# Half of the second MLP layer's outputs by Strassen's seven block products, with tokens as rows, in turn with ordinary output chunks

## The chip, the core and the metric

The kernel runs on one core of a Trainium2 chip. The metric is the time of one execution on the device in microseconds (us); shorter is better. The engines are named as the profile names them: TensorE (PE; its weight loads PEld), VectorE (DVE), ScalarE (ACT), GpSimd (POOL) and SyncE (SP), which issues the loads.

## The reference

Two layers of a decoder trunk over 256 tokens of width 2048, all in float32. Each layer has a mixer (layer 0: a convolution module beside differential attention; layer 1: a gated short convolution), a cross-attention into 256 memory tokens, and the MLP that the change touches:

```python
D_MODEL, SEQ, DEPTH, D_FF = 2048, 256, 2, 4 * 2048

def sq_relu_mlp(h, w1, w2):
    return jnp.square(jax.nn.relu(h @ w1)) @ w2

for l in range(DEPTH):
    x = x + (even_mixer if l % 2 == 0 else odd_mixer)(rms_norm(x, mix_norm_g[l]), ...)
    x = x + cross_attention(rms_norm(x, xattn_norm_g[l]), mem_n, ...)
    x = x + sq_relu_mlp(rms_norm(x, mlp_norm_g[l]), mlp_w1[l], mlp_w2[l])
return rms_norm(x, final_norm_g)
```

## The kernel before

**Layout.** The residual `x` stays in SBUF with channels as partitions: 16 tiles of 128 channels by 256 tokens. A matrix product makes one *output chunk* at a time, 128 output channels by 256 tokens, over 16 input tiles (`proj_long`, L191, and its kin).

**Three products for one.** Matmuls run on a rounded format (float32r), so each operand is split in a rounded part *hi* and a remainder *lo*, and a product is hi·hi + hi·lo + lo·hi. For weights, `weights` (L152) loads a raw tile of 128 x 1024 (512 KB) on SyncE's queue, ScalarE casts it to hi (L163), VectorE subtracts hi from raw into lo (L164). Activations lie as hi and lo next to each other (`Act`, L229), 512 columns for 256 tokens. An output chunk is 16 matmuls of a hi weight block against those 512 columns and 16 of a lo weight block against the 256 hi columns; the weight block is stationary. `residual` (L322) then adds the two halves of the PSUM bank to `x` with two VectorE additions (L325).

**Tokens as rows.** `proj_rows` (L213) does it the other way round: a 128x128 block of activations is stationary and 512 weight columns stream past it; every matmul has 512 columns.

**MLP.** `mlp` (L713) runs in four quarters of 2048 hidden units, in each of two layers, so eight in all. A quarter has 16 chunks of the first layer (each followed by the sum of its halves L209/L210, the relu and scale L720, the square L722, and the split into hi and lo, chunk by chunk, L245/L246) and 16 chunks of the second layer over these 16 tiles of hidden units, each added to `x`. In the last quarter `residual` also prepares the next norm.

**Order and buffers.** The program is unrolled; a scheduler fixes each engine's order before the run, and inserts the semaphores. Each engine works strictly in its order; a flag (`strict`) holds TensorE to the order of the program text. Tiles with the same tag share a number of slots: 5 for raw weights (`wraw`), 3 each for hi and lo weights (`wspl`), 13 large activation slots (`half`: with 4 each for the normed input and two sets of hidden units, 12 in use in the MLP). PSUM has 8 banks: 4 for chunks (`ps_mm`), 3 for attention (`ps_at`), 1 for norms (`ps_nm`).

Of the kernel before, what the change touches and what calls it, by code (L numbers as in the profile page):

```python
# [10 lines left out]
F32 = mybir.dt.float32  # L11
# [6 lines left out]
P = 128  # L18
# [27 lines left out]
def trunk(ctx: ExitStack, tc: tile.TileContext, d):  # L46
# [8 lines left out]
    prob = ctx.enter_context(tc.tile_pool(name="prob", bufs=4))  # L55
    tmp = ctx.enter_context(tc.tile_pool(name="tmp", bufs=2))
    small = ctx.enter_context(tc.tile_pool(name="small", bufs=4))
    ps_mm = ctx.enter_context(tc.tile_pool(name="ps_mm", bufs=4, space=bass.MemoryType.PSUM))
# [36 lines left out]
    def load_vec():  # L95
        nc.sync.dma_start(out=vec, in_=d["vec"][:, NG:])
        lv = vec[:, VEC["lam"] - NG:VEC["lam"] - NG + 256].rearrange("p (a b) -> p a b", a=4)
        lp = tmp.tile([P, S], F32, tag="t32", name="lp", bufs=7)[:, :128].rearrange("p (a b) -> p a b", a=2)
# [20 lines left out]
    def ordered(i, token):  # L119

        tc.stamp_issue_order_token(i.ins, token)
# [20 lines left out]
    def mm(*a, **k):  # L142
        i = T.matmul(*a, **k)  # L143
        if strict[0]:
            ordered(i, "pe")
# [3 lines left out]
        if strict[0]:  # L149
            ordered(i, "pe")  # L150

    def weights(src):  # L152
        run_later(rate[0], calls[0])
        run_stages(calls[0])
        calls[0] += 1
        raw = wraw.tile([P, 1024], F32, tag="raw", name="raw")
        hi = wspl.tile([P, 1024], F32R, tag="whi", name="whi")
        lo = wspl.tile([P, 1024], F32R, tag="wlo", name="wlo")
        n = 512 if calls[0] == 1 else 1024
        for i in range(0, 1024, n):  # L160
            o = slice(i, i + n)
            nc.sync.dma_start(out=raw[:, o], in_=src[:, o])
            A.copy(hi[:, o], raw[:, o])  # L163
            ordered(V.tensor_tensor(lo[:, o], raw[:, o], f(hi[:, o]), op=ALU.subtract), "lo")  # L164
        return hi, lo

    def wide_piece(ps, hi, lo, act, k, first, last):
# [20 lines left out]
                wide_piece(ps, hi, lo, act, g * 8, first, last)  # L188
        return pp

    def proj_long(src, act):  # L191

        ps = ps_mm.tile([P, 512], F32, tag="mm", name="mm")
        (h0, l0), (h1, l1) = [weights(src[:, g * 1024:(g + 1) * 1024]) for g in range(2)]
# [11 lines left out]
    def summed(ps):  # L206

        t = tmp32("sum")
        A.copy(t, ps[:, S:])  # L209
        V.tensor_tensor(t, ps[:, :S], t, op=ALU.add)  # L210
        return t
# [58 lines left out]
    def spread(rows):  # L270
        ps = ps_nm.tile([P, 512], F32, tag="nm", name="nmb")[:, :S]
        for t in range(2):
            dg = tmp.tile([P, P], F32, tag="diag", name="diag")
# [21 lines left out]
        return y  # L295

    def to_sbuf(ps, pool=None, name="rb"):
        r = pool.tile([P, S], F32, tag=name, name=name) if pool else tmp.tile([P, S], F32, tag="rb", name=name, bufs=3)
        A.copy(r, ps)
        return r  # L300

# [15 lines left out]
            V.tensor_tensor(self.acc, self.acc, sq, op=ALU.add)  # L317

    def tmp32(name="t32"):
        return tmp.tile([P, S], F32, tag="t32", name=name, bufs=7)  # L320

    def residual(k, ps, nxt, ss, gname):  # L322

        for i in range(2):
            V.tensor_tensor(x[:, k], x[:, k], ps[:, i * S:(i + 1) * S], op=ALU.add)  # L325
# [13 lines left out]
        return softmax_from(src, nm, width, scale)  # L339

    def softmax_from(src, bias, width, scale):
        p = tmp.tile([P, S], F32, tag="pexp", name="pexp", bufs=4)
# [9 lines left out]
    def even_mixer():  # L352
# [77 lines left out]
        def turn(h, pr):  # L430
            pt = ps_at.tile([P, 512], F32, tag="at", name="ptd")
            for t in range(2):
                for kt in range(t + 1):
                    o = kt * S + t * P
                    transpose(out=pt[:, o:o + P], in_=pr[t, 0][0][:, kt * P:(kt + 1) * P], identity=ident)
            ahl = prob.tile([P, 2, 512], F32R, tag="pt", name="ahl")
# [42 lines left out]
        def head(h):  # L479
            mem_piece(m, mss, h)  # L480
            if h == H1 - 1:
                stage(4, mem_rows)
            qkt = prob.tile([P, 2, 2, S], F32R, tag="pt", name="dqk")
# [5 lines left out]
        lsum = tmp.tile([P, S], F32, tag="lsum", name="lsum", bufs=1)  # L489

        def gated(c):
            av = summed(proj(w[c], xa))
# [149 lines left out]
    def cross(l, xa, ss, kmem):  # L642
# [20 lines left out]
        def turn(h, pr, v):  # L663
            pt = ps_at.tile([P, 512], F32, tag="at", name="ptx")
            for t in range(2):
                for kt in range(2):
                    transpose(out=pt[:, kt * S + t * P:kt * S + (t + 1) * P], in_=pr[t][:, kt * P:(kt + 1) * P],
                              identity=ident)
            pb = prob.tile([P, 2, 512], F32R, tag="pt", name="pb")
# [40 lines left out]
        return nxt, nss  # L710


    def mlp(l, xa, ss, gname):  # L713
        r = rstd(ss.acc, D)
        nxt = nss = None
        for qd in range(4):
            hid = Act(NC, "hid")
            for c in range(NC):
                u = summed(proj_long(d[f"w1{l}"][qd * NC + c], xa))
                V.scalar_tensor_tensor(u, u, 0.0, r, op0=ALU.max, op1=ALU.mult)  # L720
                u2 = tmp32("u2")
                A.activation(u2, u, AF.Square)  # L722
                hid.put(c, u2)
            if qd == 3:
                nxt, nss = Act(NC, "xn") if l == 0 else None, SumSq()
            for c in range(NC):
                ps = proj_long(d[f"w2{l}"][c][:, qd * D:(qd + 1) * D], hid)
                residual(c, ps, nxt, nss, gname)
        return nxt, nss

    xa, ss, kmem = even_mixer()
    xa, ss = cross(0, xa, ss, kmem)
    xa, ss = mlp(0, xa, ss, "mix1")
    xa, ss, kmem = odd_mixer(xa, ss)
    xa, ss = cross(1, xa, ss, kmem)
    _, ss = mlp(1, xa, ss, "final_norm_g")

    r = spread(rstd_rows(ss.acc, D))
    for g in range(8):
# [63 lines left out]
```

## Time and profile before

| | before |
|---|---|
| median of 3 runs | 2913.12 us (2912.9 to 2913.8) |
| the profiled execution | 2913.22 us, its span 2911.4 us |
| VectorE busy | 2006.7 us (69%) |
| ScalarE busy | 1471.6 us (51%) |
| DMA moved | 540.03 MB, mean 185 GB/s |
| mean granted TensorE clock | 0.998 |

How to read it: the span runs from the first to the last instruction of one execution; the profiled execution's own time is 1.8 us longer. Busy time is the time in which an engine executed instructions. In lines of groups the columns are: line, engine, operation, output<-inputs, shapes, count, then total busy us, mean ns of one, and the idle time ahead of them with what ended it. In windows they are: the window, its length, and for PE, PEld, DVE, ACT and POOL the busy us and the count, then the granted clock, the share of the DMA engines' time, and GB/s. In timelines and in the chain of waits they are: start, length, engine, line and what. Lines of DMA issues end in KB and in the median us from issue to landing.

### The profile page before, as it was taken

What the parts mean: (1) busy time and instruction counts of PE and PEld (TensorE: products, weight loads), DVE (VectorE), ACT (ScalarE), POOL (GpSimd) and SP (SyncE); (2) the same over time, 40 slices, a digit from 0 to 9 for tenths busy, and PEclk for the clock granted to TensorE, in tenths of its full rate; (3) what the DMA queues carried; (4) which work ended last, traced back from release to release, by engine and by line L of the source; (5) the groups of instructions that cost most, each with busy time, mean ns of one, the idle gap of its engine ahead of it and who ended that gap; (6) DMA issues with size and microseconds to landing.
All of it is one profiled execution on the core that took longest, in us unless ns stands there. A gap on an engine that the chain in (4) does not pass through costs nothing.

```text
span 2911.4 us, 42713 instructions
## 1 busy us (share of the span) xinstructions
PE 2891.9 (99%) x16536; PEld 2544.3 (87%) x16536; DVE 2006.7 (69%) x3180; ACT 1471.6 (51%) x2181; POOL 3.9 (0%) x20
## 2 busy tenths in 40 slices
PE   9999999999999999999999999999999999999998
PEld 7888888898888888888888888888988888888887
DVE  7899987767666656566777765467676666565665
ACT  6766455555544535445544444455555445354453
POOL 0000000000000000000000000000000000000000
PEclk9999999999999999999999999999999999999999
DMA  7464565545565665656656656655455656656564
GB/s 251 157 199 164 186 196 186 172 147 181 186 191 188 190 190 188 192 188 189 184 194 197 203 193 195 193 188 171 139 188 188 188 189 189 190 189 191 188 189 137
DMA packets 150395, 540.03 MB, mean 185 GB/s; under 512 B 16688, under 2 KB 16816, under 8 KB 150192
## 3 DMA queue, kind: packets, MB, share of 16 engines
q1 hardware_dynamic: 150192, 537.30, 58.0%
q8 instruction: 130, 2.13, 0.3%
q14 instruction: 73, 0.60, 0.1%
HBM read 535.13 MB, written 2.10 MB: 185 GB/s over the span
## 4 chain that ended last, share of the span: by engine, by line
PE 99%; DVE 0%; DMA 0%; ACT 0%; issue 0%; DVEq 0%; SPq 0%; ACTq 0%
PE mm L143 89%; PE mmr L143 8%; PE pox L143 1%; PE sx L143 1%; PE nmb L143 0%; PE nmr L143 0%; PE sc L143 0%; PE po L143 0%; DVE x L741 0%; PE ptx L148 0%; DMA x<-xT 0%; PE ptd L148 0%; ACT xn L255 0%; DVE x L325 0%; DVEq L798 0%
## 5 line engine op out<-in xcount | busy, mean ns | idle before, releaser
L164 DVE TENSOR_TENSOR wlo<-raw,whi 128x1024 fp32r<-128x1024 f32 (+1 forms) x1009 | 1234.2, 1223 | 718.6 <-issue 318.3
L163 ACT CAST whi<-raw 128x1024 fp32r<-128x1024 f32 (+1 forms) x1009 | 1061.6, 1052 | 721.3 <-PE mm L143 594.0
L143 PE MATMUL mm<-xn,whi 128*128 128x512 f32 x3840 | 937.0, 392 | 0.0
L143 PEld LDWEIGHTS mm<-xn,whi 128*128 128x128 f32 x3840 | 702.0, 188 | 133.2
L143 PEld LDWEIGHTS mm<-xn,wlo 128*128 128x128 f32 x3840 | 500.7, 191 | 23.8
L143 PE MATMUL mm<-xn,wlo 128*128 128x256 f32 x3840 | 508.4, 282 | 0.0
L143 PE MATMUL mm<-hid,whi 128*128 128x512 f32 x2048 | 489.8, 391 | 0.0
L143 PEld LDWEIGHTS mm<-hid,whi 128*128 128x128 f32 x2048 | 377.0, 188 | 72.8
L209 ACT COPY sum<-mm 128x256 f32<-128x256 f32 x272 | 101.2, 372 | 604.6 <-PE mm L143 604.4
L143 PEld LDWEIGHTS mm<-hid,wlo 128*128 128x128 f32 x2048 | 262.6, 191 | 10.0
L143 PE MATMUL mm<-hid,wlo 128*128 128x256 f32 x2048 | 265.7, 283 | 0.0
L210 DVE TENSOR_TENSOR sum<-mm,sum 128x256 f32<-128x256 f32 x272 | 115.2, 423 | 105.3 <-ACT sum L209 104.8
L325 DVE TENSOR_TENSOR x<-x,mm 128x256 f32<-128x256 f32 x384 | 160.6, 418 | 14.6 <-PE mm L143 7.9
L143 PE MATMUL mmr<-whi,mem 128*128 128x512 f32 x512 | 137.3, 390 | 0.0
L143 PE MATMUL mm<-mem,whi 128*128 128x512 f32 x512 | 126.3, 393 | 0.0
L143 PE MATMUL mm<-o,whi 128*128 128x512 f32 x512 | 124.7, 392 | 0.0
L505 DVE SCALAR_TENSOR_TENSOR cv<-a,vec,cv 128x255 f32<-128x255 f32 (+14 forms) x240 | 111.4, 464 | 2.9
L143 PEld LDWEIGHTS mmr<-whi,mem 128*128 128x128 f32 x512 | 95.8, 188 | 19.6
L143 PEld LDWEIGHTS mm<-o,whi 128*128 128x128 f32 x512 | 93.7, 188 | 18.6 <-DVE o L252 0.9
L143 PEld LDWEIGHTS mm<-mem,whi 128*128 128x128 f32 x512 | 93.1, 188 | 17.3
L143 PE MATMUL mmr<-wlo,mem 128*128 128x512 f32 x256 | 78.8, 389 | 0.0
L143 PEld LDWEIGHTS mm<-mem,wlo 128*128 128x128 f32 x512 | 67.6, 190 | 3.8
(165 smaller groups left out, 1780.2 us busy)
## 6 DMA issues: line engine op xcount, KB each, us to landing
raw<-w SPq DMA_DIRECT2D x512, 512.0 KB, 3.9
raw<-odd_in SPq DMA_DIRECT2D x96, 512.0 KB, 4.4
raw<-even_in SPq DMA_DIRECT2D x64, 512.0 KB, 4.3
raw<-xk SPq DMA_DIRECT2D x64, 512.0 KB, 4.2
raw<-xv SPq DMA_DIRECT2D x64, 512.0 KB, 3.6
raw<-xq SPq DMA_DIRECT2D x64, 512.0 KB, 4.0
raw<-xo SPq DMA_DIRECT2D x64, 512.0 KB, 3.9
raw<-even_out SPq DMA_DIRECT2D x32, 512.0 KB, 4.2
```

The lines of the kernel that those rows point to most:

```text
L143: i = T.matmul(*a, **k)
L163: A.copy(hi[:, o], raw[:, o])
L164: ordered(V.tensor_tensor(lo[:, o], raw[:, o], f(hi[:, o]), op=ALU.subtract), "lo")
L209: A.copy(t, ps[:, S:])
L210: V.tensor_tensor(t, ps[:, :S], t, op=ALU.add)
L325: V.tensor_tensor(x[:, k], x[:, k], ps[:, i * S:(i + 1) * S], op=ALU.add)
L505: ordered(V.scalar_tensor_tensor(cv[:, c, s:], a[:, c, :S - s], col("conv_a_w", i + j), cv[:, c, s:], op0=ALU.mult, op1=ALU.add), "lo")
```

## The change

In six of the eight quarters (the first three of each layer) the 16 second-layer chunks are made in another way. The eight chunks of the upper half of the channels (8 to 15) stay as they were. The 1024 channels of the lower half are computed with tokens as rows by the Strassen–Winograd scheme of seven block products. The matrix of 256 tokens x 2048 hidden units is cut in 2 x 2 blocks (128 tokens; even and odd tiles of hidden units), the weights in 2 x 2 blocks (even and odd tiles; two halves of 512 columns). Each of eight steps takes one pair of hidden tiles: seven products, each of three matmuls of 512 columns (hi·hi, lo·hi, hi·lo), 21 in all, into seven PSUM banks that stay open over all eight steps. After each step comes one ordinary chunk, in the eighth bank (`ps_nm`); TensorE is held to this order.

What belongs to it:

- the hidden units are split into hi and lo four chunks at a time, and `SevenAct.combine` forms and splits the sums and differences of their blocks;
- `seven_weights` loads the weights of a step in two tiles, in runs of 1 KB, and forms and splits the weight blocks, five of seven of them sums or differences; three of its tiles (`b22`, `tw`) have one slot;
- `seven_sum` adds the seven banks to `x` at the end of a quarter;
- `turned` transposes the lower half of `x` to token rows before the first quarter's second layer and back in the last quarter;
- in the ordinary chunks between steps, the lo part of the second half of the weights is not made by VectorE: ScalarE writes -raw, rounded, and a DMA issued by GpSimd adds the weights onto it from DRAM;
- some buffers shrink: `t32` 7 to 6 slots, `rb` 3 to 2, `diag` 2 to 1, `pexp` 4 to 3; the tiles that only the attention uses live in a pool opened around it, and the MLP's new tiles in one around the MLP.

The core of the diff:

```diff
-    def weights(src):
+    def weights(src, added=False):
...
             nc.sync.dma_start(out=raw[:, o], in_=src[:, o])
             A.copy(hi[:, o], raw[:, o])
-            ordered(V.tensor_tensor(lo[:, o], raw[:, o], f(hi[:, o]), op=ALU.subtract), "lo")
+            if added:
+                A.activation(lo[:, o], raw[:, o], AF.Copy, scale=-1.0)
+                G.dma_start(out=lo[:, o], in_=src[:, o], accum_op=ALU.add)
+            else:
+                ordered(V.tensor_tensor(lo[:, o], raw[:, o], f(hi[:, o]), op=ALU.subtract), "lo")
...
-    def proj_long(src, act):
+    def proj_long(src, act, ps=None, added=False):
...
+        (h0, l0), (h1, l1) = [weights(src[:, g * 1024:(g + 1) * 1024], added and g == 1) for g in range(2)]
...
+    class SevenAct:
+        def __init__(self, act):
+            self.act = act
+            self.t = [half.tile([P, 2, 4, 2, P], F32R, tag="half", name="hs") for _ in range(4)]
+
+        def combine(self, j, u):
+            a11, a21, a12, a22 = [u[:, :, i] for i in range(4)]
+            V.tensor_tensor(a22, a21, a22, op=ALU.add)
+            V.tensor_tensor(a21, a11, a21, op=ALU.subtract)
+            V.tensor_tensor(a11, a22, a11, op=ALU.subtract)
+            V.tensor_tensor(a12, a12, a11, op=ALU.subtract)
+            t = self.t[j]
+            A.copy(t[:, :, :, 0], u)
+            V.tensor_tensor(t[:, :, :, 1], u, f(t[:, :, :, 0]), op=ALU.subtract)
...
+    def seven_weights(src):
+        raw = [wraw.tile([P, 4, 2, P], F32, tag="raw", name="raws") for _ in range(2)]
+        for i, t in enumerate(raw):
+            nc.sync.dma_start(out=t.rearrange("p c k f -> p c (k f)"),
+                              in_=src[4 * i:4 * i + 4].rearrange("c p f -> p c f"))
+        b1, b2 = [t.rearrange("p c k f -> p k c f") for t in raw]
+        sh = wspl.tile([P, 2, 4, P], F32R, tag="whi", name="shi")
+        sl = wspl.tile([P, 2, 4, P], F32R, tag="wlo", name="slo")
+        bt = pools["mlp"].tile([P, 2, 4, P], F32R, tag="b22", name="b22", bufs=1)
+        t1, t2 = [pools["mlp"].tile([P, 2, 2, 4, P], F32R, tag=f"tw{i}", name="tw", bufs=1) for i in range(2)]
+        A.copy(sh, b1)
+        V.tensor_tensor(sl, b1, f(sh), op=ALU.subtract)
+        V.tensor_tensor(b1[:, 0], b2[:, 0], b1[:, 0], op=ALU.subtract)
+        A.copy(bt[:, 0], b2[:, 1])
+        V.tensor_tensor(b2[:, 0], b2[:, 1], b2[:, 0], op=ALU.subtract)
+        V.tensor_tensor(bt[:, 1], b2[:, 1], f(bt[:, 0]), op=ALU.subtract)
+        V.tensor_tensor(b2[:, 1], b2[:, 1], b1[:, 0], op=ALU.subtract)
+        V.tensor_tensor(b1[:, 1], b2[:, 1], b1[:, 1], op=ALU.subtract)
+        for t, b in ((t1, b1), (t2, b2)):
+            A.copy(t[:, 0], b)
+            V.tensor_tensor(t[:, 1], b, f(t[:, 0]), op=ALU.subtract)
...
+    def seven_step(pp, src, sa, s, first, last):
+        b = seven_weights(src)
+        for i, a, w in ((1, sa.single(2 * s, 0), "b11"), (2, sa.single(2 * s + 1, 0), "b21"),
+                        (5, sa.comb(1, s), "t1"), (4, sa.single(2 * s + 1, 1), "t4"), (3, sa.comb(4, s), "b22"),
+                        (7, sa.comb(3, s), "t3"), (6, sa.comb(2, s), "t2")):
+            mm(pp[i], a[0], b[w][0], start=first, stop=False)
+            mm(pp[i], a[1], b[w][0], start=False, stop=False)
+            mm(pp[i], a[0], b[w][1], start=False, stop=last)
+
+    def seven_sum(pp, acc):
+        (c11, c12), (c21, c22) = [[acc[:, i, j * 512:(j + 1) * 512] for j in range(2)] for i in range(2)]
+        u = pools["mlp"].tile([P, 512], F32, tag="u", name="u", bufs=2)
+        A.copy(u, pp[1])
+        for out, other, op in ((c11, u, ALU.add), (c11, pp[2], ALU.add), (c12, pp[5], ALU.add),
+                               (c22, pp[5], ALU.add), (c21, pp[4], ALU.subtract), (c12, pp[3], ALU.add),
+                               (u, pp[6], ALU.add), (c12, u, ALU.add), (u, pp[7], ALU.add), (c21, u, ALU.add),
+                               (c22, u, ALU.add)):
+            V.tensor_tensor(out, out, other, op=op)
+
+    def turned(rows):
...
+        for i, bank in enumerate(banks):
+            for j in range(4):
...
+                transpose(out=bank[:, j * P:(j + 1) * P], in_=src, identity=ident)
+        for i, bank in enumerate(banks):
+            A.copy(chan[:, 2 * i:2 * i + 2].rearrange("p k s -> p (k s)"), bank)
+        return toks
...
     def mlp(l, xa, ss, gname):
...
         for qd in range(4):
             hid = Act(NC, "hid")
+            sa = SevenAct(hid) if qd < 3 else None
             for c in range(NC):
...
-                u2 = tmp32("u2")
-                A.activation(u2, u, AF.Square)
-                hid.put(c, u2)
...
+                v = uu[:, c // 4 % 2]
+                A.activation(v[:, c % 4 // 2, c % 2 * 2:c % 2 * 2 + 2].rearrange("p h f -> p (h f)"), u, AF.Square)
+                if c % 4 == 3:
+                    t = hid.t[c // 4]
+                    w = v.rearrange("p a (o h) f -> p (a o) (h f)", o=2)
+                    A.copy(t[:, :, 0], w)
+                    V.tensor_tensor(t[:, :, 1], w, f(t[:, :, 0]), op=ALU.subtract)
+                    if sa:
+                        sa.combine(c // 4, v)
+                if c == 1 and qd == 0:
+                    acc = turned(True)
+                if c == 3 and qd == 3:
+                    turned(False)
+            cols = slice(qd * D, (qd + 1) * D)
+            if qd < 3:
+                pp = {i: (ps_mm if i < 5 else ps_at).tile([P, 512], F32, tag="mm" if i < 5 else "at", name=f"p{i}")
+                      for i in range(1, 8)}
+                strict[0] = True
+                for s in range(8):
+                    o = qd * D + s * 2 * P
+                    seven_step(pp, w2[:NS, :, o:o + 2 * P], sa, s, s == 0, s == 7)
+                    ps = ps_nm.tile([P, 512], F32, tag="nm", name="mmn")
+                    residual(NS + s, proj_long(w2[NS + s][:, cols], hid, ps, True), None, None, gname)
+                seven_sum(pp, acc)
+                strict[0] = False
+                continue
...
             for c in range(NC):
...
+                residual(c, proj_long(w2[c][:, cols], hid), nxt, nss, gname)
         return nxt, nss
```

More of the change, by code (lines that the diff above doesn't have):

```diff
@@ L189, in proj_group @@
         return pp
-    def proj_long(src, act):
-        ps = ps_mm.tile([P, 512], F32, tag="mm", name="mm")
-        (h0, l0), (h1, l1) = [weights(src[:, g * 1024:(g + 1) * 1024]) for g in range(2)]
+    def proj_long(src, act, ps=None, added=False):
+        if ps is None:
+            ps = ps_mm.tile([P, 512], F32, tag="mm", name="mm")
+        (h0, l0), (h1, l1) = [weights(src[:, g * 1024:(g + 1) * 1024], added and g == 1) for g in range(2)]
         w = [slice(j * P, (j + 1) * P) for j in range(8)]
@@ L272, in spread @@
         for t in range(2):
-            dg = tmp.tile([P, P], F32, tag="diag", name="diag")
+            dg = tmp.tile([P, P], F32, tag="diag", name="diag", bufs=1)
             A.activation(dg, ident, AF.Copy, scale=rows[:, t:t + 1])
@@ L297, in to_sbuf @@
     def to_sbuf(ps, pool=None, name="rb"):
-        r = pool.tile([P, S], F32, tag=name, name=name) if pool else tmp.tile([P, S], F32, tag="rb", name=name, bufs=3)
+        r = pool.tile([P, S], F32, tag=name, name=name) if pool else tmp.tile([P, S], F32, tag="rb", name=name, bufs=2)
         A.copy(r, ps)
@@ L319, in tmp32 @@
     def tmp32(name="t32"):
-        return tmp.tile([P, S], F32, tag="t32", name=name, bufs=7)
+        return tmp.tile([P, S], F32, tag="t32", name=name, bufs=6)
     def residual(k, ps, nxt, ss, gname):
@@ L488, in even_mixer @@
         cv = half.tile([P, NA, S], F32, tag="half", name="cv")
-        lsum = tmp.tile([P, S], F32, tag="lsum", name="lsum", bufs=1)
+        lsum = pools["att"].tile([P, S], F32, tag="lsum", name="lsum", bufs=1)
         def gated(c):
@@ L668, in turn @@
                               identity=ident)
-            pb = prob.tile([P, 2, 512], F32R, tag="pt", name="pb")
+            pb = pools["att"].tile([P, 2, 512], F32R, tag="pt", name="pb")
             A.copy(pb[:, 0], pt)
@@ L710, in cross, with comb, single @@
         return nxt, nss
+    NS = 8
+    class SevenAct:
[11 more added lines that the diff above has]
+            V.tensor_tensor(t[:, :, :, 1], u, f(t[:, :, :, 0]), op=ALU.subtract)
+        def comb(self, n, s):
+            return [self.t[s // 2][:, s % 2, (n - 2) % 4, i] for i in range(2)]
+        def single(self, k, t):
+            return [x(k)[:, t * P:(t + 1) * P] for x in (self.act.hi, self.act.lo)]
@@ new lines, in turned @@
+    def turned(rows):
+        chan = x[:, :NS]
+        toks = chan.rearrange("p k s -> p (k s)").rearrange("p (t c) -> p t c", t=2)
+        banks = [ps_at.tile([P, 512], F32, tag="at", name="xt") for _ in range(3)]
+        banks.append(ps_nm.tile([P, 512], F32, tag="nm", name="xtn"))
+        for i, bank in enumerate(banks):
+            for j in range(4):
+                if rows:
+                    src = chan[:, i % 2 * 4 + j, i // 2 * P:(i // 2 + 1) * P]
+                else:
+                    k = 2 * i + j // 2
+                    src = toks[:, j % 2, k * P:(k + 1) * P]
+                transpose(out=bank[:, j * P:(j + 1) * P], in_=src, identity=ident)
+        for i, bank in enumerate(banks):
+            A.copy(chan[:, 2 * i:2 * i + 2].rearrange("p k s -> p (k s)"), bank)
+        return toks
@@ L715, in mlp @@
         nxt = nss = None
+        w1, w2 = d[f"w1{l}"], d[f"w2{l}"]
+        uu = half.tile([P, 2, 2, 4, P], F32, tag="half", name="uu")
         for qd in range(4):
             hid = Act(NC, "hid")
+            sa = SevenAct(hid) if qd < 3 else None
             for c in range(NC):
-                u = summed(proj_long(d[f"w1{l}"][qd * NC + c], xa))
+                u = summed(proj_long(w1[qd * NC + c], xa))
                 V.scalar_tensor_tensor(u, u, 0.0, r, op0=ALU.max, op1=ALU.mult)
-                u2 = tmp32("u2")
@@ L726, in mlp @@
+            nxt, nss = Act(NC, "xn") if l == 0 else None, SumSq()
             for c in range(NC):
-                ps = proj_long(d[f"w2{l}"][c][:, qd * D:(qd + 1) * D], hid)
-                residual(c, ps, nxt, nss, gname)
+                residual(c, proj_long(w2[c][:, cols], hid), nxt, nss, gname)
         return nxt, nss
[L731 to L735, printed above, removed]
@@ L736, in trunk, with scoped, attentions @@
-    _, ss = mlp(1, xa, ss, "final_norm_g")
+    def scoped(name, fn, *a):
+        with tc.tile_pool(name=name, bufs=4) as pools[name]:
+            return fn(*a)
+    def attentions(first):
+        a = even_mixer() if first else odd_mixer(*state)
+        return cross(0 if first else 1, *a)
+    state = scoped("att", attentions, True)
+    state = scoped("mlp", mlp, 0, *state, "mix1")
+    state = scoped("att", attentions, False)
+    _, ss = scoped("mlp", mlp, 1, *state, "final_norm_g")
     r = spread(rstd_rows(ss.acc, D))
```

17 lines of the change are left out of this document (10 added, 7 removed).

## The prediction

> **What bounds the kernel now.** I read the page first, for who is busy and what the chain that ended last is made of; then that chain in order of time; then one stretch of the second MLP layer, as a table of windows and as a timeline; then the groups by shape for durations; last the DMA issues.
>
> ```profile
> PE 2891.9 (99%) x16536; PEld 2544.3 (87%) x16536; DVE 2006.7 (69%) x3180; ACT 1471.6 (51%) x2181; POOL 3.9 (0%) x20
> ...
> PE 99%; DVE 0%; DMA 0%; ACT 0%; issue 0%; DVEq 0%; SPq 0%; ACTq 0%
> ```
>
> TensorE is busy for 99% of the span, and the chain that ended last runs through it alone. So time is won only by fewer or shorter matmuls, and lost as soon as something makes TensorE wait. Pieces of the chain give its prices:
>
> ```profile
> 70.11 0.89 PE sc L143 x12
> 71.00 8.58 PE mm L143 x48
> 79.58 0.33 PE ptd L148 x3
> ...
> 559.78 0.44 PE ptx L148 x4
> ...
> 738.58 708.34 PE mm L143 x4070
> ...
> 1801.37 87.06 PE mmr L143 x384
> ```
>
> The piece of 708.34 us is almost the whole first MLP: 4070 matmuls with no gap. One output chunk is 32 matmuls (16 of 512 columns, 16 of 256), so a chunk takes 708.34 / 4070 x 32 = 5.57 us. The last piece is value projections with tokens as rows, where every matmul has 512 columns and another stationary block, as the seven products will: 87.06 / 384 = 0.2267 us each. A 128x128 transpose takes 0.44 / 4 = 0.11 us. How much room the other engines leave in the second MLP layer:
>
> ```profile
> 1000.00:1085.00 85.00, 85.00 (x489) 75.04 (x488) 49.40 (x62) 33.11 (x33) 0.00 (x0) 1.00 0.63 191
> ```
>
> In these 85 us TensorE never rests; VectorE is busy for 49.40 (58%), ScalarE for 33.11 (39%), the DMA engines for 63%, and the granted clock is full. One chunk of it:
>
> ```profile
> 1003.56 3.82 PE L143 MATMUL mm<-hid,whi 128*128 128x512 f32 x16
> 1004.00 1.05 ACT L163 CAST whi<-raw 128x1024 fp32r<-128x1024 f32 x1 [2.43 <-PE mm L143]
> 1004.00 0.87 DVE L325 TENSOR_TENSOR x<-x,mm 128x256 f32<-128x256 f32 x2
> 1005.08 1.23 DVE L164 TENSOR_TENSOR wlo<-raw,whi 128x1024 fp32r<-128x1024 f32 x1 [0.21 <-ACT whi L163]
> 1005.83 1.05 ACT L163 CAST whi<-raw 128x1024 fp32r<-128x1024 f32 x1 [0.78 <-PE mm L143]
> 1007.22 2.08 PE L143 MATMUL mm<-hid,wlo 128*128 128x256 f32 x16
> 1008.43 1.23 DVE L164 TENSOR_TENSOR wlo<-raw,whi 128x1024 fp32r<-128x1024 f32 x1 [2.12 <-PE mm L143]
> 1009.13 3.82 PE L143 MATMUL mm<-hid,whi 128*128 128x512 f32 x16
> ```
>
> The 512-column half takes 1007.22 - 1003.56 = 3.66 us (0.229 each), the other 1.91 us. Casts and subtractions wait for TensorE to give a slot back, not the other way round: they have slack.
>
> **The products.** A step (one of 8 in each of 6 quarters, so 48) replaces one ordinary chunk's worth of work by 21 matmuls of 512 columns: 21 x 0.2267 = 4.76 us for 5.57. A step with the ordinary chunk that follows it then needs 10.33 us of TensorE where two chunks needed 11.14. Gain 0.81 x 48 = 38.8 us, all of it on the path.
>
> **The transposes.** Eight channel tiles of the residual are turned to token rows and back, in each layer: 2 x 2 x 16 = 64 transposes x 0.11 = 7.0 us on the path. Their ScalarE copies lie under first-layer chunks. TensorE alone thus gains 31.8 us: 2913.2 - 31.8 = 2881.4, the floor.
>
> **The other engines, in a step.** Prices by shape:
>
> ```profile
> L164 DVE TENSOR_TENSOR wlo<-raw,whi 128x1024 fp32r<-128x1024 f32 x1007 | 1232.8, 1224 | 717.1 <-issue 318.3 <-PE mm L143 267.7 <-ACT whi L163 114.9
> L163 ACT CAST whi<-raw 128x1024 fp32r<-128x1024 f32 x1007 | 1060.4, 1053 | 720.1 <-PE mm L143 594.0 <-PE mmr L143 96.1 <-issue 10.5
> ...
> L325 DVE TENSOR_TENSOR x<-x,mm 128x256 f32<-128x256 f32 x384 | 160.6, 418 | 14.6 <-PE mm L143 7.9
> ...
> L246 DVE TENSOR_TENSOR hid<-u,hid 128x256 fp32r<-128x256 f32 x128 | 53.5, 418 | 1.8 <-ACT hid L245 1.8
> ...
> L252 DVE TENSOR_TENSOR o<-pox,o 128x512 fp32r<-128x512 f32 x16 | 11.0, 685 | 2.8 <-ACT o L251 2.8
> ...
> L251 ACT CAST o<-pox 128x512 fp32r<-128x512 f32 x16 | 9.3, 584 | 4.3 <-PE pox L143 4.3
> ```
>
> VectorE: the seven blocks need three operations of 1024 (3 x 1.224) and five of 512 (5 x 0.685) = 7.1 us; the ordinary chunk needs one subtraction (1.224; the second is given to a DMA) and two residual additions (0.87): together 9.2 us of 10.33, 89%, where before it was 58%. A 512-wide sum of two SBUF tiles has no row; 256 wide costs 0.418 from PSUM and from SBUF alike, so I take 0.685. ScalarE: three casts of 1024 and one of 512 (3.74), two casts for the chunk (2.11), one negated copy (at 1.05): 6.9 us of 10.33. Neither is over the period, but VectorE has only 1.1 us left, and it works strictly in its order.
>
> What order asks of it: the tiles of the combined weights exist once. Counting from a step's first matmul, the fourth-block tile is free after 15 matmuls (3.4 us), the first pair after 12 (2.7), the second pair after 21 (4.8). The new split of the fourth block waits on VectorE for a cast, which waits for those 15 matmuls; behind it stand the next two differences, the splits of both pairs, and the residual additions. After 3.4: a 512 cast, three 512 operations, a 1024 cast, a 1024 subtraction: 0.58 + 3 x 0.685 + 1.05 + 1.22 = 4.9, done at 8.3. The first pair's remainder is first read by the ninth matmul of the next step, at 10.33 + 8 x 0.2267 = 12.1. Slack 3.8 us, into which the ordinary subtraction (1.22) and the second pair's (1.22) may still fall. So no wait from this, as taken; uncovered, each 1 us late costs 48.
>
> A tighter loop runs over the five load slots, which are asked for in order, four to a step: the second load of the next step takes the slot that the first load of this step gives up, and that one is held until the first pair is split.
>
> ```profile
> raw<-w SPq DMA_DIRECT2D x512, 512.0 KB, 3.9
> ...
> memraw<-memT SPq DMA_DIRECT2D x16, 256.0 KB, 3.1
> ...
> gvec<-vec SPq DMA_DIRECT2D x1, 64.0 KB, 1.9
> ```
>
> A load lands 3.9 us after its issue; then five 512 operations (3.4), a cast (1.05), a subtraction (1.22): 9.6 us round the loop, against 10.33. Margin 0.7, out of which come the handovers (0.21 from cast to subtraction in the timeline above). Behind the waiting load on SP's queue stand the two loads of the ordinary chunk. I take 0.1 us a step for it, 5 us; the bounds are 0 and, with one 1024 subtraction caught inside the loop (9.6 + 1.2 = 10.8), 0.5 x 48 = 24.
>
> **DMA.** Five moves of 0.524 MB a step (the remainder of one ordinary half is made by a second read that adds onto a negated copy): 2.62 MB in 10.33 us = 254 GB/s. The most that this trace shows over some microseconds:
>
> ```profile
> 15.00:20.00 5.00, 5.00 (x23) 4.16 (x23) 5.00 (x10) 5.00 (x10) 0.00 (x0) 1.00 1.03 405
> ```
>
> 254 of 405 GB/s leaves room. The weights of the seven products come in runs of 1 KB instead of 4 KB. Rows of 512 B (the 64 KB load above, 1.9 us) land no later than their size asks for, beside 3.1 us for 256 KB and 3.9 for 512 KB; I take nothing, and 15% more on these loads as the upper bound (0.2 us of 9.6 in the loop, within its margin).
>
> The adding DMA has no row: no load from GpSimd and none that adds is in this trace. Its slot comes free when the previous ordinary chunk ends, at 0 in a step's count; two ScalarE operations (2.1) come first; the remainder is read by the last eight 256-column matmuls of this step's chunk, from 4.76 + 3.66 + 0.95 = 9.4 on. So it may take 7.3 us. The nearest row is the plain load, 3.9; twice that, since it reads two operands, is 7.8. I take a value between, nearer to the plain load, so no wait; the bounds are 0 and 0.5 us a step (24 us). Nothing else is queued on GpSimd. [...]
>
> **Hidden units in fours.** They are now split four chunks at a time, not one. The chain after a chunk, from the timeline around the start of a first-layer chunk's successor:
>
> ```profile
> 914.50 2.68 PE L143 MATMUL mm<-xn,whi 128*128 128x512 f32 x11
> 914.93 0.37 ACT L209 COPY sum<-mm 128x256 f32<-128x256 f32 x1 [2.68 <-PE mm L143]
> ...
> 915.34 0.42 DVE L210 TENSOR_TENSOR sum<-mm,sum 128x256 f32<-128x256 f32 x1 [0.32 <-ACT sum L209]
> 915.79 0.42 DVE L720 SCALAR_TENSOR_TENSOR sum<-sum,rb 128x256 f32<-128x256 f32 x1
> 916.25 0.42 ACT L722 ACTIVATE u<-sum 128x256 f32<-128x256 f32 x1
> ```
>
> The square is there 2.17 us after the chunk's end (916.67 - 914.50); then a cast of 1024 (1.05) and a subtraction of 1024 (1.22): 4.4 us. In the two quarters that stay ordinary, the next chunk reads unit 12 at its thirteenth matmul, 12 x 0.229 = 2.7 us in: TensorE waits 1.7 us, twice, 3.4 us; with a weight cast and a subtraction in between (2.3 more) up to 8. In the six others the step's 4.76 us lie ahead of that chunk, need at 7.5: nothing, and at worst 0.
>
> **The rest at nothing, with its cover.** The sums of neighbours for the products: per four chunks 4 x 0.418 + 1.224 = 2.9 us of VectorE; a first-layer chunk then costs it 2 x 1.224 + 2 x 0.42 + (1.224 + 2.9) / 4 = 4.3 of 5.57 us. The final additions of a quarter: 11 x 0.685 = 7.5 us, beside the last ordinary chunk and the next first-layer chunk; uncovered, 7.5 - 5.57 = 2 us x 6 = 12. The one PSUM bank for ordinary chunks: its two additions (0.87) end inside the next step's 4.76. One exponential tile less (three for the four of a differential head): ScalarE waits once a head for the first pair to be combined, and between a head's scores and its transposes TensorE has 8.58 us of other work (first three rows of the chain); uncovered, one 256-wide operation for each of 8 heads, 0.42 x 8 = 3. The entry into a step phase: the first split blocks need 7.1 us of VectorE beside the last first-layer chunks, which leave 1.2 us each; I take 0, and as the upper bound one chunk's work left over, 5.6 us x 6 = 34, since I can't tell how early they start.
>
> **Sum.** 2913.2 - 38.8 + 7.0 + 5 (load loop) + 3.4 (hidden in fours) = 2889.8, call it 2890. It is made against the profiled execution, 2913.22 us (span 2911.4 and 1.8 around it), 0.1 over the median 2913.12. That is 0.8% faster.
>
> **Rivals.**
> First, some of the waits that I set to nothing come due, but less than the gain: one subtraction caught inside the load loop (+24 - 5), or the adding DMA at twice a plain load (+24), or part of the entries (up to 34). One of the first two alone gives 2890 + 19 to 24, 2909 to 2914; half of one gives 2900. For it: VectorE's idle share falls from 42% to 11%. Against it: the loops close with 0.7 us or more.
>
> Second, slower: VectorE's order sets the step. If both 1024 subtractions that are not part of the loop (the ordinary one and the second pair's) fall between the landing of the second load and the release of its slot, the loop takes 9.6 + 2.4 = 12.0 us. Then a step is 1.7 us over 10.33: 2913.2 - 31.8 + 3.4 + 1.7 x 48 = 2966. It decides from 10.33 + (31.8 - 3.4) / 48 = 10.92 us a step on; the table of windows would show TensorE at 86% in these stages (10.33 of 12.0), and VectorE at 77% with waits for DMA. For it: the order of VectorE is fixed ahead of the run. Against: 4 us of each loop are load time, into which 0.87 + 1.22 + 1.22 fit.
>
> Third, the change doesn't reach its price: 21 products at the pace of an ordinary 512-column matmul, 0.229, would cost 0.05 us more a step, 2 us in all. That cannot turn the sign. [...]
>
> **How the numbers follow.** This kernel's runs lie within 2912.9 to 2913.8, so about 0.2% (5.8 us) is what can be told from no change. My forecast (2881 to 2900) gets 0.50, the first rival 0.25 (of it 0.15 below 2907.3 and 0.10 above), the second and the late adding DMA together 0.25. Faster 0.50 + 0.15 = 0.65, the same 0.10, slower 0.25. The range begins at the floor, 2881, less 1 for the spread, 2880, and goes up into the second rival until no more than 2 in 10 is left out: at 2930, where a step takes 11.3 us. The forecast's own range is 2881 to 2900.
>
> **What would show it.** In the changed profile: some 64 transposes more and 48 x 11 matmuls fewer; steps of 4.76 us; a step and a chunk every 10.3 to 10.5 us; VectorE at 85 to 90% in the step stages; the adding DMA landing in 4 to 7 us; two gaps of 1.7 us or more where the last quarters turn to the second layer. I am wrong if a step takes more than 10.9 us (then the releaser of TensorE's waits, VectorE, a load or the adding DMA, says which loop), or if gaps at the six entries exceed 3 us each.

## The result, and the profile after

The changed kernel takes 3023.1 us (median; 3020.29 to 3026.17) against 2913.01: ratio 1.0378, 95% interval 1.036 to 1.0396. I had forecast 2890: it is 110 us slower than the kernel before and 133 us over the forecast. From the page of the changed kernel, the lines that answer to those of before:

```profile
span 3019.1 us, 42397 instructions
...
PE 2903.0 (96%) x16072; PEld 2521.6 (84%) x16072; DVE 2206.7 (73%) x3414; ACT 1605.4 (53%) x2275; POOL 45.0 (1%) x68
...
q0 software_dynamic: 6912, 25.17, 4.3%
...
PE 80%; DMA 14%; ACT 3%; DVE 2%; issue 1%; SPq 0%; ACTq 0%; DVEq 0%; POOLq 0%
PE mm L143 66%; DMA wlo<-w 13%; PE mmr L143 7%; PE mmn L143 3%; PE p L143 2%; ACT wlo L166 1%; PE pox L143 1%; PE sx L143 1%; ACT whi L164 1%; DVE wlo L169 0%; PE nmb L143 0%; ACT tw L776 0%; DVE slo L768 0%; DVE cv L511 0%; PE nmr L143 0%
```

The chain that ended last was TensorE for 99%; now 13% of it is one kind of transfer, `wlo<-w`, the DMA that GpSimd issues to add the weights onto the negated copy. The chain in order of time shows it once in every step (start, length, what), here in the first quarter and at its end:

```profile
839.91 9.90 DMA wlo<-w
853.66 8.38 DMA wlo<-w
865.92 8.19 DMA wlo<-w
877.99 8.08 DMA wlo<-w
889.95 8.35 DMA wlo<-w
902.18 8.46 DMA wlo<-w
915.30 8.92 DMA wlo<-w
928.11 9.57 DMA wlo<-w
939.74 84.54 PE mm L143 x480
```

Eight issues, 88.2 us from the first to the last: 12.6 us a step with its chunk, where I had reckoned with 10.33 to 10.5 and two chunks took 11.14. TensorE's wait for it, over all 48 steps (total us, times, longest):

```profile
PE mmn L143 <- DMA wlo<-w: 72.1, 46, 3.7
```

The timeline of one step says what fills it:

```profile
887.17 0.40 PE L143 MATMUL mmn<-hid,whi 128*128 128x512 f32 x1
...
887.40 0.62 PE L143 MATMUL p<-shi,hid 128*128 128x512 f32 x2
...
887.64 1.05 ACT L164 CAST whi<-raw 128x1024 fp32r<-128x1024 f32 x1 [2.28 <-issue]
...
888.60 1.06 ACT L166 ACTIVATE wlo<-raw 128x1024 fp32r<-128x1024 f32 x1
...
889.95 0.84 POOL L167 DMA_DIRECT2D wlo<-w  x1 [11.10 <-ACT wlo L166]
...
895.58 1.11 PE L143 MATMUL mmn<-hid,wlo 128*128 128x256 f32 x8
...
898.35 1.22 PE L143 MATMUL mmn<-hid,wlo 128*128 128x256 f32 x8 [1.65 <-DMA wlo<-w]
...
899.40 0.40 PE L143 MATMUL mmn<-hid,whi 128*128 128x512 f32 x1
```

It is a closed loop. The chunk of the step before ends at 887.40 and gives back the slots of its second half, hi and remainder; ScalarE casts into the one (to 888.60) and writes the negated copy into the other (to 889.66); GpSimd issues at 889.95; the DMA lands at 898.34, 8.4 us later; TensorE, which waited 1.65 us for it, does the last eight 256-column matmuls and one more, and at 899.63 the next chunk's slot is free: 0.24 + 0.96 + 1.06 + 0.29 + 8.39 + 1.29 = 12.23 us. Nothing of the seven products is in it, by this timeline; the profile's own chain passes through five of their matmuls to ScalarE's queue instead, and the runs that change ScalarE's order, below, bear on which is right. The mean of 12.6 is longer still, as the granted clock fell after some of these waits: it was 0.50 from 912 to 914 us, and the nine matmuls behind the DMA that landed at 910.64 took 2.24 us (2.02 behind the eighth) where those behind the other six took 1.45. The DMA issues (median us to landing last) set the price beside plain loads of the same size:

```profile
raw<-w SPq DMA_DIRECT2D x416, 512.0 KB, 4.0
raws<-w SPq DMA_DIRECT2D x96, 512.0 KB, 3.9
...
wlo<-w POOLq DMA_DIRECT2D x48, 512.0 KB, 8.5
```

That is not all: the chain shows the first MLP's start 14.2 us later than before (`mm` x456 from 667.13 where it was 652.94), so attention had become slower too, and the first steps of each quarter are longer than the others.

### The profile page after: what moved, and what is told of

It is laid out like the page before. It is cut to its first block, busy times and chain, and to the rows that moved or that the text cites. A ratio compares the mean times of both kernels' runs of the same rounds, so it can differ in the third digit from the quotient of the medians.

```text
span 3019.1 us, 42397 instructions
## 1 busy us (share of the span) xinstructions
PE 2903.0 (96%) x16072; PEld 2521.6 (84%) x16072; DVE 2206.7 (73%) x3414; ACT 1605.4 (53%) x2275; POOL 45.0 (1%) x68
## 4 chain that ended last, share of the span: by engine, by line
PE 80%; DMA 14%; ACT 3%; DVE 2%; issue 1%; SPq 0%; ACTq 0%; DVEq 0%; POOLq 0%
PE mm L143 66%; DMA wlo<-w 13%; PE mmr L143 7%; PE mmn L143 3%; PE p L143 2%; ACT wlo L166 1%; PE pox L143 1%; PE sx L143 1%; ACT whi L164 1%; DVE wlo L169 0%; PE nmb L143 0%; ACT tw L776 0%; DVE slo L768 0%; DVE cv L511 0%; PE nmr L143 0%
## 5 line engine op out<-in xcount | busy, mean ns | idle before, releaser
L169 DVE TENSOR_TENSOR wlo<-raw,whi 128x1024 fp32r<-128x1024 f32 (+1 forms) x865 | 1057.0, 1222 | 457.5 <-PE mm L143 169.6
L164 ACT CAST whi<-raw 128x1024 fp32r<-128x1024 f32 (+1 forms) x913 | 958.4, 1050 | 667.4 <-PE mm L143 271.6
L143 PE MATMUL mmn<-hid,whi 128*128 128x512 f32 x768 | 192.1, 392 | 0.0
L143 PE MATMUL mmn<-hid,wlo 128*128 128x256 f32 x768 | 116.1, 296 | 72.2 <-DMA wlo<-w 72.1
L143 PEld LDWEIGHTS mmn<-hid,wlo 128*128 128x128 f32 x768 | 104.5, 196 | 85.7 <-DMA wlo<-w 81.9
L143 PEld LDWEIGHTS mmn<-hid,whi 128*128 128x128 f32 x768 | 145.3, 189 | 28.2
L777 DVE TENSOR_TENSOR tw<-raws,tw 128x1024 fp32r<-128x1024 f32 x96 | 114.2, 1220 | 41.3 <-ACT tw L776 41.3
L143 PE MATMUL p<-tw,hs 128*128 128x512 f32 x432 | 120.4, 402 | 13.1 <-ACT tw L776 6.9
L143 PE MATMUL mm<-hid,whi 128*128 128x512 f32 x512 | 122.7, 391 | 0.0
L143 PEld LDWEIGHTS mm<-hid,whi 128*128 128x128 f32 x512 | 94.1, 188 | 18.6 <-DVE hid L841 0.5
```

Of the source, the lines that this page charges most:

```text
L777: V.tensor_tensor(t[:, 1], b, f(t[:, 0]), op=ALU.subtract)
```

## The experiments

Times are medians, each beside the kernel before on the same chip; ratios with 95% intervals.

| run | us | ratio |
|---|---|---|
| the change | 3023.10 | 1.0378 [1.036, 1.0396] |
| e1_no_adding_dma | 2927.02 | 1.0045 [1.003, 1.006] |
| e2_copy_first | 3025.56 | 1.0387 [1.037, 1.0403] |
| e3_second_slot | 2979.99 | 1.0232 [1.0215, 1.0249] |
| e4_before_small_buffers | 2928.70 | 1.0054 [1.0039, 1.0069] |
| e5_full_buffers | 2911.93 | 0.9995 [0.9986, 1.0004] |
| e6_early_first | 2904.30 | 0.9969 [0.9956, 0.9982] |
| e7_forced_order | 2990.46 | 1.0274 [1.0256, 1.0291] |
| e8_plain_load | 2942.64 | 1.0097 [1.0082, 1.0112] |
| e9_late_combine | 2889.43 | 0.9916 [0.9902, 0.9929] |
| e10_gpsimd | 2961.33 | 1.0162 [1.0149, 1.0176] |

**Theory A** is the loop above. **Rival B**: VectorE's order or the load slots set the step, and the DMA only shows up in the chain because it happens to come last. **Rival C**: the extra traffic delays everything else.

**e1_no_adding_dma**

```diff
-                    residual(NS + s, proj_long(w2[NS + s][:, cols], hid, ps, True), None, None, gname)
+                    residual(NS + s, proj_long(w2[NS + s][:, cols], hid, ps), None, None, gname)
```

> The change, but VectorE makes every remainder of the ordinary weights by subtraction again; no adding DMA. Theory A (the loop through the slot of the added remainder sets the step: chunk end, two ScalarE copies, a DMA that lands after 8.4 us, eight matmuls; 12.6 us a step in the profile): the loop is gone, the step falls to what TensorE (10.33) and VectorE (9.2 + 1.2 = 10.4) allow, about 10.6 with gaps, so 3023 - 48 x 2.0 = about 2927 us. Rival B (VectorE's order or the load slots set the step anyhow): VectorE has 1.2 us more to do in each step, so no gain, 3023 to 3080 us. Rival C (the adding DMA only burdens the DMA engines and delays the loads): also faster, as A.

Measured 2927.02: 96 us less than the change, the number that A and C gave. B is out: VectorE has more to do and the steps are shorter. The chain of this run, from the third step of a quarter on, and a window over those six steps:

```profile
862.30 4.78 PE p L143 x21
867.08 5.55 PE mmn L143 x32
872.63 4.78 PE p L143 x21
877.41 5.55 PE mmn L143 x32
```

```profile
862.30:924.00 61.70, 61.70 (x318) 52.95 (x318) 58.63 (x75) 31.93 (x34) 0.00 (x0) 1.00 0.61 205
```

Step and chunk take 4.78 + 5.55 = 10.33 us, TensorE's floor, with VectorE busy for 58.63 of 61.70 us: 95%, and still TensorE waits for nothing in this stretch.

**e2_copy_first, e7_forced_order**

```diff
             if added:
                 A.activation(lo[:, o], raw[:, o], AF.Copy, scale=-1.0)
                 G.dma_start(out=lo[:, o], in_=src[:, o], accum_op=ALU.add)
+            A.copy(hi[:, o], raw[:, o])
```

> The change with one move: in the weights with the adding DMA, ScalarE writes the negated copy and GpSimd issues the DMA ahead of the cast to hi, not behind it. Theory A: one cast of 1.05 us leaves the loop, 48 x 1.05 = 50 us faster, about 2973 us. Rivals B and C: same work, same bytes, no change, 3023 us.

3025.56, no change, but this tells nothing of A: its timeline still has the cast first. The scheduler had kept its order, and moving lines in the program text was not a move on the engine. With a token that fixes the order of the two ScalarE operations:

```diff
-                A.activation(lo[:, o], raw[:, o], AF.Copy, scale=-1.0)
+                ordered(A.activation(lo[:, o], raw[:, o], AF.Copy, scale=-1.0), "act")
                 G.dma_start(out=lo[:, o], in_=src[:, o], accum_op=ALU.add)
+                ordered(A.copy(hi[:, o], raw[:, o]), "act")
```

> The second experiment again, since its edit left ScalarE's order as it was (cast, then negated copy): now the order of the two is fixed, negated copy and DMA first. Theory A (slot loop of the adding DMA): one cast leaves the loop, 48 x 1.05 = 50 us faster than 3023, about 2973 us. Rival B or C (VectorE, load slots or DMA traffic): 3023, no change.

2990.46: 33 us less than the change, two thirds of the 50. Over the six quarters the 42 intervals between GpSimd's issues shrank from 12.57 to 11.74 us in the mean (in the first quarter of this run the issues go from 838.18 to 923.29, where the change went from 839.91 to 928.11). That is 0.83 of the cast's 0.96 us, so the cast was in the loop, and 42 x 0.83 = 35 us (between these two profiled executions the whole difference is 40 us; this run's four executions lie from 2980 to 2997). B and C had said no change.

**e3_second_slot**

```diff
-        lo = wspl.tile([P, 1024], F32R, tag="wlo", name="wlo")
+        lo = (pools["mlp"].tile([P, 1024], F32R, tag="wla", name="wlo", bufs=1) if added == 2 else
+              wspl.tile([P, 1024], F32R, tag="wlo", name="wlo"))
...
+                    residual(NS + s, proj_long(w2[NS + s][:, cols], hid, ps, 1 + s % 2), None, None, gname)
```

> The change, but the added remainder goes in every second step to a slot of its own, so that its DMA can start a step earlier (room is made by taking the scratch tile of the final additions from the raw weight slots). Theory A: the loop spans two steps, the wait for the DMA vanishes, the step falls to 10.4 to 10.8 us, about 2920 to 2937 us. Rival B: 3023, no change. Rival C: bytes unchanged, 3023, no change.

2979.99: 43 us less, against C, but at most half of what A had promised (86 to 103). Who waits for whom (total us, times, longest) in this run, and two pieces of its chain:

```profile
ACT wlo L167 <- DMA raw<-w: 106.4, 24, 6.4
...
PEld mmn L143 <- DMA wlo<-w: 34.4, 20, 2.7
...
859.59 2.35 DVE tw L778 x2
861.97 8.23 DMA raw<-w
```

With one loop opened, the next one closes: the negated copy now waits for its raw weights. Their load starts when VectorE has split the pairs of combined weights and so given a load slot back, and it then takes 8.2 us, where I had reckoned with 3.9. That is the loop of my prediction that I had given 0.7 us of room; a DMA that starts earlier needs its source earlier. The loads of the weights are slower in this run altogether (median 4.7 and 5.2 us, where the change has 4.0 and 3.9), so here C, the traffic, has a part that was not separated from the slots.

**e8_plain_load**

```diff
-                G.dma_start(out=lo[:, o], in_=src[:, o], accum_op=ALU.add)
+                G.dma_start(out=lo[:, o], in_=src[:, o])
```

> The change, but GpSimd's DMA copies the weights over the remainder instead of adding them to the negated copy: same place, same queue, same bytes from DRAM, no addition (so the lo part of these weights is the weights themselves, not the remainder). If it is the adding that makes the DMA take 8.4 us: it lands in about 4.5 us, the loop falls under the period, and the time comes to about 2927 us, that of the first experiment. If it is GpSimd's path or the traffic: 8 us and 3010 to 3023 us.

2942.64: 80 us less than the change, 16 us more than e1. Its shortest steps are at 10.33 us, but the 42 intervals between GpSimd's issues are 10.89 us in the mean, and TensorE still waits for this DMA 11 times, 10.5 us in all. From this run's page and issues:

```profile
q0 software_dynamic: 6912, 25.17, 2.4%
...
wlo<-w POOLq DMA_DIRECT2D x48, 512.0 KB, 6.4
```

This run leaves out the adding alone: the remainder is then not one, and only its time is read. Without the adding the DMA lands 2.1 us earlier, between the 4.5 us that I expected if the adding was all of it and the 8 if it was none, and takes 2.4% instead of 4.3% of the DMA engines' time for the same bytes. Some 2 us more than a plain load (6.4 against 4.5 and 3.9 on SyncE's queue in this run) are there without adding. Whether GpSimd's path, the type of the tile it writes (fp32r, where the loads write f32) or the place in the step (right behind other loads) causes them was not tried. The traces' records of single packets say where the time passes, not why. In the changed kernel the first packet of such a DMA starts 4.7 us after the issue (median of 48), while SyncE's loads keep the DMA engines 81% busy, and its packets then take 3.4 us; in this run it is 2.8 and 3.2 us, and in e7, which adds too, 2.8 and 4.9. So the 2.1 us can't be put down to the moving of the added bytes alone, and why the first packet starts 4.7 us after the issue in one run and 2.8 us in the others was not shown. At 6.4 us the loop is 10.2, just under the period, which is why so small a difference decided 80 us.

**e4_before_small_buffers, e5_full_buffers**

```diff
-            dg = tmp.tile([P, P], F32, tag="diag", name="diag")
+            dg = tmp.tile([P, P], F32, tag="diag", name="diag", bufs=1)
...
-        p = tmp.tile([P, S], F32, tag="pexp", name="pexp", bufs=4)
+        p = tmp.tile([P, S], F32, tag="pexp", name="pexp", bufs=3)
```

(and `t32` 7 to 6, `rb` 3 to 2.) e5 is e1 with these four edits undone and, to make the room, the scratch tile `u` of a quarter's final additions taken from the raw weights' slots.

> The kernel before with only the shrunken buffers of the change (t32 6, rb 2, diag 1, pexp 3); no products, no pools. In the profile of the changed kernel the first MLP begins 14.2 us later than before. If the buffers cause it: about 2913 + 14 (layer 0) and less in layer 1, 2925 to 2930 us. If it comes from the pools or elsewhere: 2913, no change.

> The first experiment's kernel (no adding DMA, 2927 us) with the four shrunken buffers back at their old size (t32 7, rb 3, diag 2, pexp 4; the scratch tile of the final additions comes from the raw weight slots to make room). If the shrunken buffers cost 15 us there as they did in the kernel before (2928.7 against 2913.3): 2912 us, level with the kernel before. If that cost was covered elsewhere: 2927, no change.

In the kernel before, the small buffers alone cost 15.4 us (2928.70 against 2913.30); put back in the first experiment's kernel they give back 15.1 (2927.02 to 2911.93). TensorE's waits in the fourth experiment:

```profile
PE nmb L143 <- ACT diag L274: 11.7, 14, 2.9
PE mmr L143 <- ACT whi L163: 6.3, 1, 6.3
PE ptd L148 <- DVE pexp L427: 2.2, 4, 1.0
```

The first was 2.9 us, once, in the kernel before; the third was not there. `spread` makes two diagonal tiles and a matmul from each; with one slot the second waits for the first's matmul. That is 8.8 us, the exponentials 2.2; the rest of the 15 is not assigned to one of the four.

**e6_early_first, e9_late_combine**

(e6, on top of e5:)

```diff
+                if sa and c == 10:
+                    ready = seven_weights(w2[:NS, :, qd * D:qd * D + 2 * P])
                 u = summed(proj_long(w1[qd * NC + c], xa))
```

> As the run with full buffers, but the weights of a quarter's first step are loaded and split ahead of the eleventh first-layer chunk, not after the sixteenth. In the first experiment's trace a quarter's first two steps took 9.0 and 6.4 us where the others take 4.78, 5.8 us too much, six times: 35 us. If the late start of the weight chain is the cause: 2912 - 6 x 4 to 5.8 = 2877 to 2888 us. If VectorE is simply full there (the chain's 7.1 us of it are then paid in the first-layer chunks): 2912, no change.

2904.30, 8 us of the 24 to 35 expected: the first step of each quarter now takes 4.78 us, but the second waits (its chain: VectorE from 831.4 to 836.4, one operation after the other). So both were true: the weight chain started late, and VectorE is full at the entry. Then:

```diff
-                        sa.combine(c // 4, v)
+                        if c // 4 < 3:
+                            sa.combine(c // 4, v)
+                        else:
+                            last = v
...
+                    if s == 4:
+                        sa.combine(3, last)
```

> As the run with the early first step (2904 us), but the sums of the last four hidden chunks (2.9 us of VectorE, first read by the seventh step) are formed after the fourth step instead of before the first. In that run's trace VectorE is full from 822 to 840 us and TensorE waits 2.1 us in the second step, after which its granted clock is low: the step is 4.0 us (first quarter) and 2.5 us too long, 18 us over six quarters. If VectorE's load at the entry is the cause: about 2886 to 2892 us. If the second step waits for something else (loads, slots): 2904, no change.

2889.43: the middle of what was expected, 24 us faster than the kernel before, 8 us over the floor. TensorE's waits for the new tiles are 0.2 us in all:

```profile
PE mm L143 <- ACT whi L164: 0.8, 1, 0.8
PE mm L143 <- DVE wlo L169: 0.8, 2, 0.4
PE p L143 <- DVE tw L777: 0.2, 1, 0.2
```

This version (no adding DMA, full buffers, early first weights, late last sums) beats both kernels.

**e10_gpsimd**

```diff
-            V.tensor_tensor(a22, a21, a22, op=ALU.add)
+            G.tensor_tensor(a22, a21, a22, op=ALU.add)
```

(in e9, and likewise the other three sums of `combine`.)

> The same, and GpSimd instead of VectorE forms the sums of hidden units (four 256-wide operations per four chunks, the splits stay on VectorE): 1.7 us of VectorE less per four chunks. If VectorE is what is short at the entries: at least as fast as the run before, about 2884 to 2888 us, near the floor of 2881. [...]

2961.33, 72 us slower than e9. VectorE and GpSimd operations of its timeline, and two waits:

```profile
759.51 0.73 POOL L740 TENSOR_TENSOR uu<-uu 128x256 f32<-128x256 f32 x1 [559.35 <-DVE hid L844]
759.70 1.62 DVE L169 TENSOR_TENSOR wlo<-raw,whi 128x1024 fp32r<-128x1024 f32 x1 [0.34 <-PE mm L143]
...
760.32 1.59 POOL L741 TENSOR_TENSOR uu<-uu 128x256 f32<-128x256 f32 x1
...
761.99 0.74 POOL L742 TENSOR_TENSOR uu<-uu 128x256 f32<-128x256 f32 x1
```

```profile
ACT hs L745 <- POOL uu L743: 108.6, 24, 5.4
...
PE mm L143 <- ACT whi L164: 30.4, 12, 3.2
```

The first and the third sum take GpSimd 0.73 and 0.74 us where VectorE took 0.42; the second, which starts 0.62 us into a VectorE subtraction, takes 1.59, and that subtraction takes 1.62 instead of 1.23. Why both take longer there was not shown. The four sums follow each other, ScalarE's cast of their result waits up to 5.4 us for them, and the weight casts stand behind it in ScalarE's order; TensorE waits 30.4 us for them, and its mean granted clock is 0.989 where e9 has 0.998.

## Why the prediction was wrong

**The step that failed** is the adding DMA: "I take a value between, nearer to the plain load, so no wait; the bounds are 0 and 0.5 us a step (24 us)". It landed after 8.5 us, over my upper row (7.8, twice a plain load), and the room was not 7.3: I had left out the handovers, 0.24 from the chunk's end to ScalarE and 0.29 from ScalarE to GpSimd, so 6.8. I had also put all sixteen hi matmuls ahead of the DMA's readers; the kernel does the sixteenth last, so that 1.29 us follow the landing and not 0.95. The measured loop leaves 10.33 - (12.23 - 8.39) = 6.5. My own sign of being wrong, a step over 10.9 us, came up with this DMA as the releaser. The price of it is what e1 gives back, 96 us, four times my bound: once the loop is longer than the period, the whole excess is paid in every step, and its landing time varies upward (8.1 to 9.9 in the first quarter) with no slack to absorb it. Part of the price is the clock that falls after the waits: the mean granted clock is 0.990 in the changed kernel's profile and 0.995 in e1's, by an estimate 0.005 x 3019 = 15 us. Why the DMA takes 8.5 us is open, as said under e8. The right form would have been to write out this loop as I did that of the load slots.

**Small buffers**: I priced one of four, the exponential tile, at nothing with 3 us as its bound, and passed over the single diagonal tile, though two of them are filled in turn. Measured 15.4 us. The tile sits in the norms, outside the MLP that the change is about, and TensorE waited for it 14 times.

**The entries**: "I take 0, and as the upper bound ... 34". Without the adding DMA and with full buffers, 2911.93 - 2881.5 (the floor from 2913.3) leaves 30.4 us. In the first experiment's chain a quarter's first two steps take 9.0 and 6.4 us instead of 4.78. The mechanism was the one that I named, the value the wrong end of the range.

**The sum.** From the floor: 2881.5 + 30.4 (entries) + 15.1 (buffers) + 96.1 (adding DMA) = 3023.1. Each term is a difference of two runs, so the sum closes by itself; what tests it is that the buffers cost nearly the same in the kernel before (15.4), and that the late sums and the early weights take back 22.5 of the 30.4 (2911.93 - 2889.43). The other 8 us are not assigned.

**What held.** The products take 4.78 us (predicted 4.76), 16 transposes 1.31 + 0.44 = 1.75 (1.76), the 1 KB runs cost nothing (3.9 us to landing, beside 4.0 for the 4 KB runs). VectorE carried even the subtraction taken from it: 58.63 / 6 = 9.8 us a step (reckoned 9.2 + 1.2 = 10.4; operations that don't wait for one another start 0.60 us apart where one alone takes 0.68: 879.81 and 880.41 in the changed kernel's timeline). Two terms of the sum came to nothing: the load loop (5 us) did not bind at 10.33 us in e1, and the hidden units in fours (3.4 us) showed no gap in the ordinary quarters (no wait of a matmul for them is in e9's trace). The slower rival gave 2966 and put the blame on VectorE's order; the sign was its, the mechanism was not. And the version in which the three failed terms are removed takes 2889.43. That this is nearly the 2890 of the forecast is chance: 8.4 us of the forecast are the two terms that came to nothing, and this version is 8 us over the floor for other reasons.

## What to carry to other kernels

Work that is moved to an idle resource must be priced by the loop that it closes, with every handover: who gives back its buffer, how long until the result is there, who then waits. With one slot, a transfer of 8.4 us in a 10.3 us period became the period. Before an operation is taken off a busy engine, see whether it was late there: VectorE at 95% without it kept TensorE waiting for nothing in the steady steps. When buffers are shrunk to make room, look for tags that one helper takes twice in a row.

## What the runs showed of the hardware

TensorE's granted clock fell from 1.00 to 0.50 after waits of about 2 us. In the first experiment TensorE did little from 837 to 840 us, and the window table then has (granted clock third from the end):

```profile
839.00:840.00 1.00, 0.31 (x3) 0.01 (x1) 1.00 (x2) 0.97 (x3) 0.00 (x0) 1.00 1.09 226
840.00:841.00 1.00, 1.00 (x3) 0.81 (x4) 1.00 (x2) 0.85 (x1) 0.00 (x0) 0.57 0.61 205
841.00:842.00 1.00, 1.00 (x4) 0.81 (x3) 1.00 (x2) 0.00 (x0) 0.00 (x0) 0.50 0.84 287
842.00:843.00 1.00, 1.00 (x3) 0.75 (x3) 1.00 (x2) 0.00 (x0) 0.00 (x0) 0.50 0.80 250
843.00:844.00 1.00, 1.00 (x5) 0.78 (x4) 1.00 (x3) 0.62 (x1) 0.00 (x0) 0.72 0.84 283
844.00:845.00 1.00, 1.00 (x6) 0.83 (x5) 1.00 (x3) 0.00 (x0) 0.00 (x0) 1.00 0.95 334
```

Two waits of 1.15 and 0.69 us were followed by some 3.5 us at about half clock: 13 matmuls took 4.83 us. In e6 a wait of 2.1 us comes once in each of the six quarters; in the first layer it did the same in the first quarter (the same 13 matmuls took 4.84 us) and not in the other two (3.25 and 3.26). So where the clock fell, 1.6 us were lost behind a wait of about 2: it fell behind 1.84 us of waiting in two pieces and behind 2.08 in one, and not behind two other waits of 2.1. What decides between them was not shown.
